# Seven of eight expert quads scattered to rows in memory and gathered back by token, in a GDN + MoE layer on one core

## The chip, the cores and the metric

One core of one Trainium2 chip. The metric is device microseconds for one execution of the whole program, the median of several runs. One execution is taken with the hardware profiler; its time and its span stand beside the runs.

## The reference

One encoder layer over 512 tokens of width 1024, float32: a gated delta mixer, a residual LayerNorm, a hierarchical mixture of experts, a second residual LayerNorm, and a gated projection. The change touches what lies from the first LayerNorm to the second.

```python
x = _layernorm(ALPHA * x + gdn_mixer(x), ln_g[0], ln_b[0])       # ALPHA = 2 ** 0.25
g_onehot = one_hot(argmax(x @ w_group + b_group), 4)             # 1 of 4 groups
e = (x @ w_router + b_router)[chosen group]                      # 8 experts of that group
top_val, top_idx = top_k(e, 2)
top_w = softmax(top_val) * p_group                               # two weights per token
for each chosen expert (w_gate, w_up 1024x256, w_down 256x1024):
    h += top_w * ((silu(x @ w_gate) * (x @ w_up)) @ w_down)
x = _layernorm(ALPHA * x + h, ln_g[1], ln_b[1])
x = x + sigmoid(x @ pe_w_gate) * (p @ pe_w_proj)
```

There are 32 experts and two per token, so 1024 pairs of a token and an expert.

## The kernel before

P is 128 and D 1024; the tokens lie as four chunks `c` of 128 rows in `x1` (also called `z`). The first 700 us or so compute the mixer; there the change only drops four loads and adds a small copy.

**First LayerNorm (`apply`, `store`).** Each chunk is normalised on ACT, given gain and bias by POOL (L859, L860, 128x512 each; one chunk by DVE, L853, L854), stored to the table `x1d` in DRAM (L863), and then scaled by ALPHA on ACT (L865).

**Routing.** A chain of small operations on DVE finds each token's two experts and its slot. The experts form eight quads `q` of four; an expert has 32 slots in each of two tiles `t`, so a quad has 256 slots. `table()` makes the token number of each slot, `gim` (L1083). What doesn't fit its slots goes to an overflow loop over a list (`ntot`, `elist`, `gio`); with these inputs the list is empty. Behind `gim` the same DVE stream computes that list, the two weights `cw` and the weight by quad and token `cq` (L1125 to L1191).

**Experts.** The weights come in 96 tiles of 1 MB, twelve a quad (eight for `up`, four for `down`), through a ring of 16 slots; `load()` (L798, on SP's queue) issues the next tile at each step and waits until its slot is free. `fetch(q)` gathers the 256 rows of a quad from `x1d` with two indirect DMAs on POOL (L952) into a tile `E`, two quads ahead. `flip_x` transposes them, `up` multiplies with gate and up weights, step `kt` of eight (L1223 on PE), while `stage` copies the next tile's four expert blocks into `ws`, three on DVE (L1216) and one on ACT (L1218), with two buffers. `down` multiplies with the down weights, and `split` leaves the result as a high and a low part (L1279, L1280). The result is brought to its tokens by one-hot matrices `oh` (L1268): `combine` makes four matmuls (L1306) for each chunk and half, and `add` accumulates on DVE with the weight `cq` (L1311). These eight pieces of quad q are the list `fill`, one at each step of `up(q + 1)`.

**Order.** From quad 0 on the order on each engine is the order in the code (`in_order`), and so it is in the routing for all but SP. Elsewhere a scheduler sets it.

**Tail.** The gate weights (`w<-in_pe_g`) are split into high and low parts on ACT and POOL (L1405, L1406); then come the second LayerNorm (`norm`, L1412 to L1421) and the gate matmuls L1435. `project_p` (L914, stored as `pjd`) is done early, in pieces around the routing as `NPJ` says.

Of the kernel before, what the change touches and what calls it, by code (L numbers as in the profile page):

```python
# [44 lines left out]
SO = (1, 2, 0, 3)  # L45
TE = 'V'
NPJ = (0, 1, 1)
LNV = (1,)
# [13 lines left out]
TC = 256  # L62


@with_exitstack
def program(ctx: ExitStack, tc: tile.TileContext, a: dict, out: bass.AP):
# [45 lines left out]
    dramp = ctx.enter_context(tc.tile_pool(name="dramp", bufs=1, space=bass.MemoryType.DRAM))  # L112

# [474 lines left out]
    def finish(qt, get):  # L588
# [13 lines left out]
        t = wk.tile([P, 2, NC_, 2], F32, name="rq2")  # L602
# [245 lines left out]
    def apply(c, y, nm, ny):  # L848

        if c in LNV:  # L850
            for n in range(2):
                ns = slice(512 * n, 512 * n + 512)
                V.scalar_tensor_tensor(x1[:, c, ns], x1[:, c, ns], nm, lng[n], op0=OP.add, op1=OP.mult)  # L853
                V.scalar_tensor_tensor(x1[:, c, ns], x1[:, c, ns], y, lng[2 + n], op0=OP.mult, op1=OP.add)  # L854
        else:
            A.activation(x1[:, c], x1[:, c], AF.Identity, bias=ny, scale=y)
            for n in range(2):
                ns = slice(512 * n, 512 * n + 512)
# [28 lines left out]
    for c in SO:  # L887
        store(c)
        if R0 > RA:
            after(stored[-1], early[-1])  # L890
# [57 lines left out]
    def fetch(q):  # L948

        xg = ab_pool.tile([P, 2, D], F32, name="E")  # L950
        for t in range(2):
            i = nc.gpsimd.indirect_dma_start(out=xg[:, t], out_offset=None, in_=x1d[:, :],  # L952
                                         in_offset=bass.IndirectOffsetOnAxis(ap=gim[:, 2 * q + t:2 * q + t + 1], axis=0))
        fetched.append(i)
        return xg
# [107 lines left out]
    def table(slot, col, nm, e):  # L1063
# [19 lines left out]
        V.tensor_copy(gi, gf)  # L1083

        def numbers():
            yf = rtile((16,), "yf")
            V.tensor_scalar(yf, pln[:, 2], 0.0, None, op0=OP.is_equal)
            V.scalar_tensor_tensor(gf, yf, 1.0e5, gf, op0=OP.mult, op1=OP.add)
            if nm == "o":
                V.tensor_scalar(pln[:, 2], pln[:, 2], -1.0, 0.0, op0=OP.add, op1=OP.max)  # L1090
                V.scalar_tensor_tensor(gf, pln[:, 2], 512.0, gf, op0=OP.mult, op1=OP.add)
        return gi, gf, numbers
# [3 lines left out]
    gim, gfm, numbers = table(s128, col, "m", V if TE == "V" else G)  # L1096
# [5 lines left out]
    numbers()  # L1102
# [14 lines left out]
    e2 = rtile((NC_, 1), "e2")  # L1117
    V.tensor_sub(e2, m2, m1)
    A.activation(ge, ge, AF.Exp)
    A.activation(e2, e2, AF.Exp)  # L1120


    NL = 16
    lim = rtile((1, 32), "lim")
    V.tensor_scalar(lim, pre, -32.0, 160.0, op0=OP.mult, op1=OP.add)  # L1125
    V.tensor_scalar(lim, lim, 32.0, None, op0=OP.max)
    nb = rtile((1, 32), "nb")
    V.tensor_sub(nb, prk[:, NC_:], lim)
    nbi = rtile((1, 32), "nbi", I32)
    V.tensor_scalar(nbi, nb, 0.0, 127.0, op0=OP.max, op1=OP.add)  # L1130
    V.tensor_scalar(nbi, nbi, 7, None, op0=OP.arith_shift_right)
    V.tensor_copy(nb, nbi)
    cum = rtile((2, 1, 32), "cum")
    V.tensor_copy(cum[:, 0], nb)
    for j in range(5):
        s_, d_ = cum[:, j % 2], cum[:, 1 - j % 2]
        o = 1 << j
        V.tensor_copy(d_[:, :, :o], s_[:, :, :o])
        V.tensor_add(d_[:, :, o:], s_[:, :, o:], s_[:, :, :32 - o])
    inc = cum[:, 1]  # L1140
    exc = rtile((1, 32), "exc")
    V.tensor_sub(exc, inc, nb)
    ntot = per.tile([P, 1], I32, name="ntot")
    V.tensor_copy(ntot, inc[:, 0, 31:32])
    tlim = rtile((2, NC_), "tlim")
    of_token(tlim, lim.to_broadcast([P, NC_, 32]), t32)
    texc = rtile((2, NC_), "texc")
    of_token(texc, exc.to_broadcast([P, NC_, 32]), t32b)
    V.tensor_sub(tlim, rank, tlim)
    oi = rtile((2, 2, NC_), "bi", I32)  # L1150
    V.tensor_copy(oi[:, 0], tlim)
# [92 lines left out]
    def up(q, xgT, js, ws, fill):  # L1244
# [4 lines left out]
        for kt in range(KT):  # L1249
# [10 lines left out]
            if fill:  # L1260
                fill.pop(0)()
# [9 lines left out]
    def down(q, hT, js, ws, fill, ys):  # L1271
# [11 lines left out]
        for n in range(2):  # L1283
# [14 lines left out]
            if fill and q < 7:  # L1298
                fill.pop(0)()
# [289 lines left out]
```

## Time and profile before

| what | value |
|---|---|
| median of 3 runs | 1116.09 us (1110.93 to 1119.45) |
| the profiled execution | 1118.27 us, its span 1116.5 us |
| busy share of the span | PE 90%, DVE 72%, ACT 49%, POOL 30% |
| mean granted TensorE clock | 0.942 of full |
| from HBM, to HBM | 174.77 MB read, 12.65 MB written |

The stages by the trace: mixer to about 700 us, first LayerNorm to 736, routing to 754, quad 0 from 769, quad 1 from 799, last expert matmul 1038.7, tail to 1116.5. A busy share is a mean over these stages; the sections below read single stages. The granted clock is 1.00 at the 2.4 GHz level and 0.50 at the 1.2 GHz level. A group of "busy, mean ns of one" is followed by the idle time of its engine in front of it and by what ended it.

### The profile page before, as it was taken

How to read it: one execution, taken by the hardware profiler on the slowest of the kernel's cores; microseconds unless marked ns; L12 is line 12 of the kernel's file. 1: busy time of each engine (PE TensorE's matmuls, PEld its weight loads, DVE VectorE, ACT ScalarE, POOL GpSimd, SP SyncE). 2: the span in 40 equal slices, each digit the busy share in tenths (PEclk: the TensorE clock that was granted, in tenths of full speed). 3: DMA queues.
4: the chain of work that ended last, by engine and by line, in shares of the span. 5: the costliest groups of instructions: out<-in, count | busy, mean ns of one | idle time of the engine just before them, and what ended most of it. 6: DMA issues, size and time to landing. Idle time of an engine off the chain costs nothing. (4 is left out here: it accounts for less than half of the span.)

```text
span 1116.5 us, 19701 instructions
## 1 busy us (share of the span) xinstructions
PE 1009.3 (90%) x6954; PEld 703.5 (63%) x6954; DVE 809.4 (72%) x1834; ACT 548.3 (49%) x1406; POOL 334.3 (30%) x273
## 2 busy tenths in 40 slices
PE   9876798977979999989999999958999999999688
PEld 7755677765868887778877888833333333333377
DVE  5889997999894778996556322697666666666784
ACT  3455566655574777556586343224443334432321
POOL 1544534232234344424240274052000000000452
PEclk7988899987999998999999999969999999999789
DMA  4324232121123313223154234878999999970401
GB/s 150 108 66 124 85 98 65 49 57 29 48 90 124 91 58 117 92 77 111 61 161 145 88 123 132 340 274 309 415 420 419 420 406 393 393 319 38 190 28 48
DMA packets 80117, 188.71 MB, mean 169 GB/s; under 512 B 15345, under 2 KB 36849, under 8 KB 67345
## 3 DMA queue, kind: packets, MB, share of 16 engines
q1 hardware_dynamic: 77712, 179.05, 44.1%
q0 software_dynamic: 2304, 8.39, 2.0%
q8 instruction: 55, 0.90, 0.3%
q14 instruction: 46, 0.37, 0.1%
HBM read 174.77 MB, written 12.65 MB: 168 GB/s over the span
## 5 line engine op out<-in xcount | busy, mean ns | idle before, releaser
L240 POOL TENSOR_TENSOR wl<-wr,wh 128x512 fp32r<-128x512 f32 x120 | 160.8, 1343 | 322.8 <-PE pin L243 136.6
L243 PE MATMUL pin<-xh,wh 128*128 128x512 f32 x448 | 137.1, 426 | 36.1 <-DVE cv L257 29.1
L243 PE MATMUL pin<-xl,wh 128*128 128x512 f32 x448 | 135.2, 419 | 0.0
L243 PE MATMUL pin<-xh,wl 128*128 128x512 f32 x448 | 131.2, 412 | 0.3 <-POOL wl L240 0.3
L243 PEld LDWEIGHTS pin<-xh,wh 128*128 128x128 f32 x448 | 86.4, 202 | 57.6 <-DVE cv L257 12.6
L238 ACT ACTIVATE wh<-wr 128x512 fp32r<-128x512 f32 x120 | 75.8, 632 | 92.5 <-PE pin L243 41.2
L1218 ACT ACTIVATE ws<-w 128x512 f32 x96 | 60.5, 630 | 111.8 <-PE ps L1223 57.9
L1216 DVE COPY ws<-w 128x512 f32 x288 | 105.7, 424 | 9.4 <-issue 3.5
L257 DVE SCALAR_TENSOR_TENSOR cv<-pin,cvw,cv 128x510 f32<-128x510 f32 (+1 forms) x128 | 94.4, 741 | 14.8 <-ACT cv L254 14.0
L243 PEld LDWEIGHTS pin<-xl,wh 128*128 128x128 f32 x448 | 89.1, 202 | 19.4 <-DVE xl L642 0.2
L243 PEld LDWEIGHTS pin<-xh,wl 128*128 128x128 f32 x448 | 87.2, 198 | 19.1 <-POOL wl L240 0.7
L952 POOL DMA_INDIRECT E<-x1d,gim x16 | 16.2, 1013 | 170.3 <-PE ps L1206 157.0
L446 POOL TENSOR_TENSOR dc<-dc,negm 128x512 f32<-128x512 f32 x32 | 47.0, 1473 | 44.3 <-DMA dc<-gcd 18.9
L397 DVE TENSOR_TENSOR x<-x,tmp 128x30 f32<-128x30 f32 (+14 forms) x120 | 56.3, 469 | 2.1
L395 DVE TENSOR_TENSOR tmp<-x 128x30 f32<-128x30 f32 (+14 forms) x120 | 53.5, 446 | 2.1
L1311 DVE SCALAR_TENSOR_TENSOR x<-pin,cq,x 128x512 f32<-128x512 f32 x36 | 26.9, 750 | 36.4 <-PE pin L1306 33.0
L448 ACT ACTIVATE dc<-dc,lb 128x128 f32<-128x128 f32 x128 | 41.6, 399 | 15.2 <-POOL dc L446 14.2
L1435 PE MATMUL ps<-w 128*128 128x512 f32 (+1 forms) x192 | 46.4, 405 | 0.0
L542 DVE SCALAR_TENSOR_TENSOR r<-ps,negc,nv 128x128 f32<-128x128 f32 x96 | 29.0, 344 | 23.3 <-PE ps L539 23.1
L1435 PEld LDWEIGHTS ps<-w 128*128 128x128 f32 x192 | 37.5, 206 | 7.6
L1223 PE MATMUL pin<-ws,AT 128*32 128x512 f32 x256 | 39.8, 593 | 0.8 <-DVE ws L1216 0.8
L538 PE MATMUL ps<-st,kcm 128*128 128x256 f32 x96 | 31.7, 413 | 9.6 <-DVE st L570 5.6
(460 smaller groups left out, 2164.7 us busy)
## 6 DMA issues: line engine op xcount, KB each, us to landing
w<-in_w_gu SPq DMA_DIRECT2D x64, 1024.0 KB, 10.0
w<-in_w_dn SPq DMA_DIRECT2D x32, 1024.0 KB, 8.4
wr<-in_w_in SPq DMA_DIRECT2D x96, 256.0 KB, 2.7
dc<-gcd SPq DMA_DIRECT2D x32, 256.0 KB, 3.4
wr<-in_w_out SPq DMA_DIRECT2D x24, 256.0 KB, 3.0
zd<-th SPq DMA_DIRECT2D x16, 256.0 KB, 2.5
zs<-zd SPq DMA_DIRECT2D x16, 256.0 KB, 2.7
w<-in_pe_g SPq DMA_DIRECT2D x6, 512.0 KB, 5.9
```

What stands on the lines that cost most here:

```text
L238: A.activation(wh, wr, AF.Copy)
L240: G.tensor_tensor(wl, wr, wh.bitcast(F32), op=OP.subtract)
L243: T.matmul(ps, w[:, k], parts[k0 + k][n], start=(k0 + k + n == 0 and w is wh), stop=(k0 + k == nk_ - 1 and w is wl))
L257: V.scalar_tensor_tensor(y[:, lo:hi], ps[:, lo + j - 2:hi + j - 2], cvw[:, m, j:j + 1], y[:, lo:hi], op0=OP.mult, op1=OP.add)
L395: V.tensor_tensor(t, X[:, m + 1:, m:m + 1].to_broadcast([P, n, m]), X[:, m:m + 1, :m].to_broadcast([P, n, m]), op=OP.mult)
L397: V.tensor_tensor(X[:, m + 1:, :m], X[:, m + 1:, :m], t, op=OP.add)
L446: G.tensor_tensor(dc, dc, negm[:, d:d + 1].to_broadcast([P, 4, P]), op=OP.add)
L448: A.activation(dc[:, u], dc[:, u], AF.Exp, bias=lb[:, c, u0 + u:u0 + u + 1])
L1216: V.tensor_copy(ws[:, p:p + 1], src)
L1218: A.activation(ws[:, p:p + 1], src, AF.Copy)
L1223: T.matmul(ps[32 * j:32 * j + 32], l[:, 32 * j:32 * j + 32], w[:, j], start=first, stop=last, skip_group_check=True)
L1435: T.matmul(pg[n][:, 0:w], x_[:, kt], w_[kt][:, 512 * n + o:512 * n + o + w], start=(kt == 0 and m == 0), stop=(kt == KT - 1 and m == 2))
```

## The change

Quads 0 to 6 (`MQ` = 7) no longer use the one-hot combine. `down` copies its result on ACT into a tile `yr` (tag `AT`), and two indirect DMAs on POOL scatter the 256 rows to a table `yd` in DRAM, row 256 q + slot. The row numbers `rows_w` of empty slots are out of bounds, and such rows are skipped; the gathers of `fetch` now skip empty slots in the same way. `yd` is filled with zeros by fourteen DMAs of 512 KB on SP's queue; its last row, filled by one more, is what a token reads for a choice that lies in quad 7 or in the overflow list. At quad 7 `collect` gathers for each chunk and each of the two choices the rows of the 128 tokens (eight indirect DMAs), and eight DVE operations add them with the weight `cw`, one at each step of `up(7)`. Quad 7 keeps the combine.

`x1` and `x1d` hold bare normalised rows: gain and bias are applied per feature in `flip_x`, where a feature is a partition (`gbT`), and the residual is put together later by sixteen DVE operations (`residual`), four a quad in quads 3 to 6, from a broadcast of the LayerNorm gain and bias (1 MB, loaded at quad 2).

The list calculations become a generator `later`, of which a piece runs at each step of `up` in quads 0 and 1. `project_p` moves (`NPJ`): two chunks ahead of the rank sums, one ahead of the table, one behind.

```diff
-NPJ = (0, 1, 1)
+NPJ = (2, 3, 3)
+MQ = 7
+    yd = dramp.tile([256 * MQ + 1, D], F32, name="yd")
+    gbT = lgp.tile([P, KT, 2], F32, name="gbT")
+    V.tensor_copy(gbT, wrg[:, :, 36:38])
-    lng = [hd.tile([P, S], F32, name="kkq", bufs=BKK) for _ in range(4)]
-    for i in range(4):
-        nc.sync.dma_start(lng[i], a["ln"][:, i // 2, 512 * (i % 2):512 * (i % 2) + 512].to_broadcast([P, 512]))
     def apply(c, y, nm, ny):
-        if c in LNV:
...
-        else:
-            A.activation(x1[:, c], x1[:, c], AF.Identity, bias=ny, scale=y)
-            for n in range(2):
-                ns = slice(512 * n, 512 * n + 512)
-                G.tensor_tensor(x1[:, c, ns], x1[:, c, ns], lng[n], op=OP.mult)
-                G.tensor_tensor(x1[:, c, ns], x1[:, c, ns], lng[2 + n], op=OP.add)
+        A.activation(x1[:, c], x1[:, c], AF.Identity, bias=ny, scale=y)
     def store(c):
         stored.append(nc.sync.dma_start(x1d[c * P:(c + 1) * P, :], x1[:, c]))
-        A.activation(x1[:, c], x1[:, c], AF.Copy, scale=ALPHA)
...
-                                         in_offset=bass.IndirectOffsetOnAxis(ap=gim[:, 2 * q + t:2 * q + t + 1], axis=0))
+                                         in_offset=bass.IndirectOffsetOnAxis(ap=gim[:, 2 * q + t:2 * q + t + 1], axis=0),
+                                         bounds_check=S - 1, oob_is_err=False)
...
     xg = [fetch(0)]
     for i in range(R1, RA + RB):
         after(load(), fetched[0], True)
+    zer = rt.tile([P, 512], F32, name="zer")
+    G.memset(zer, 0.0)
+    after(nc.sync.dma_start(yd[256 * MQ:, :].rearrange("o (r e) -> o r e", e=512),
+                            zer[0:1, None, :].to_broadcast([1, 2, 512])), fetched[1], True)
+    for i in range(2 * MQ):
+        nc.sync.dma_start(yd[P * i:P * i + P, :].rearrange("p (r e) -> p r e", e=512),
+                          zer[:, None, :].to_broadcast([P, 2, 512]))
...
+    def later():
+        V.scalar_tensor_tensor(yfm, yfm, 1.0e5, VAL[:, 0, 0:1].to_broadcast([P, 16]), op0=OP.mult, op1=OP.add)
+        V.scalar_tensor_tensor(rows_w, IO32[:, 0:16], 128.0, yfm, op0=OP.mult, op1=OP.add)
...
+        V.tensor_scalar(rows_r, no, 256.0 * MQ, None, op0=OP.min)
...
     def flip_x(xg):
...
-            A.activation(xgT[:, 2 * k2:2 * k2 + 2], pt, AF.Copy)
+            for i in range(2):
+                kt = 2 * k2 + i
+                A.activation(xgT[:, kt], pt[:, i], AF.Identity, scale=gbT[:, kt, 0:1], bias=gbT[:, kt, 1:2])
+    def residual(lng):
+        def part(c, n, k):
+            z_ = z[:, c, 512 * n:512 * n + 512]
+            if k:
+                V.scalar_tensor_tensor(z_, lng[:, 2 + n], ALPHA, z_, op0=OP.mult, op1=OP.add)
+            else:
+                V.scalar_tensor_tensor(z_, lng[:, n], ALPHA, z_, op0=OP.mult, op1=OP.mult)
+        return [lambda c=c, n=n, k=k: part(c, n, k) for c in range(NC_) for n in range(2) for k in range(2)]
     def down(q, hT, js, ws, fill, ys):
+        if q < MQ:
+            yr = ab_pool.tile([P, 2, D], F32, name="AT")
         def split(n, py):
+            if q < MQ:
+                for t in range(2):
+                    A.activation(yr[:, t, 512 * n:512 * n + 512], py[t], AF.Copy)
+                return
...
+        for t in range(2 if q < MQ else 0):
+            nc.gpsimd.indirect_dma_start(
+                out=yd[:, :], out_offset=bass.IndirectOffsetOnAxis(ap=rows_w[:, 2 * q + t:2 * q + t + 1], axis=0),
+                in_=yr[:, t], in_offset=None, bounds_check=256 * MQ - 1, oob_is_err=False)
         return ws
+    def collect():
+        gs_ = [ab_pool.tile([P, 2, D], F32, name="E") for _ in range(2)] + [ring([P, 2, D]) for _ in range(2)]
+        for c in range(NC_):
+            for k in range(2):
+                nc.gpsimd.indirect_dma_start(
+                    out=gs_[c][:, k], out_offset=None, in_=yd[:, :],
+                    in_offset=bass.IndirectOffsetOnAxis(ap=rows_r[:, k, c:c + 1], axis=0))
+        def part(c, k):
+            V.scalar_tensor_tensor(z[:, c], gs_[c][:, k], cw[:, k, c:c + 1], z[:, c], op0=OP.mult, op1=OP.add)
+        return [lambda c=c, k=k: part(c, k) for c in range(NC_) for k in range(2)]
...
     for q in range(8):
...
+        fill = []
+        if q < 2:
+            fill = [lambda: next(rest, None) for _ in range(8)]
+        elif q == 2:
+            for _ in rest:
+                pass
...
+            lng = e2.tile([P, 4, 512], F32, name="y")
+            nc.sync.dma_start(lng, a["ln"][:, 0:2].rearrange("o k (n w) -> o (k n) w", n=2).to_broadcast([P, 4, 512]))
+        elif q < 7:
+            fill = res_parts[:4]
+            del res_parts[:4]
+        if q == 2:
+            res_parts = residual(lng)
+        if q == 7:
+            fill = collect()
         h = up(q, xgT, js, ws, fill)
...
-        oh = slots(q)
+        if q >= MQ:
+            oh = slots(q)
...
-        fill = [lambda q=q, c=c, n=n, y=y, oh=oh: add(q, c, n, combine(oh, y, c, "ps1" if q % 2 else "pin"))
-                for n, y in enumerate(ys) for c in range(NC_)]
```

On DVE, between the routing and the first staging copies of quad 0, the end of the list calculations (`hot` and `ef` to `elist`, `gp`, `den`) stands ahead of the copies before:

```order
L1167 TENSOR_REDUCE ef<-hot 128x16
L1169 CAST ei<-ef 128x16
L1171 TENSOR_SCALAR elist<-ei 128x16
L1172 TENSOR_SCALAR elist<-ei 128x16
L1175 TENSOR_REDUCE gp<-ge 128x4
L1177 SCALAR_TENSOR_TENSOR den<-e_7768,gp 128x4
L1216 ISA
L1216 COPY ws<-w 128x512
```

In the changed kernel the copies on DVE come at once behind `gim` and the choice of the quads' experts, `jsel`:

```order
L1082 CAST gim<-gfm 128x16
L1104 TENSOR_TENSOR t_7660<-ROW,pre 128x32x3
L1108 TENSOR_REDUCE jr<-t_7660 128x32
L1110 CAST jsel<-jr 128x32
L1114 TENSOR_TENSOR ge<-lg,mxg 128x16
L1116 TENSOR_TENSOR e_7765<-mx_7601,mx_7589 128x4
L1263 TENSOR_LOAD jsel
L1263 ISA x6
L1242 ISA
L1242 COPY ws<-w 128x512
```

Some fifty operations moved behind these copies, into the steps of quads 0 and 1.

On POOL, from the first LayerNorm to the end of the overflow list's load, the program before has gain and bias (`kkq`), the gathers, and the split of a gate weight tile (`w<-E,w`):

```order
L859 TENSOR_TENSOR x_66<-x_66,kkq 128x512 x2
L860 TENSOR_TENSOR x_66<-x_66,kkq 128x512 x3
L952 DMA E<-x1d,gim 128x1024 x2
L1070 TENSOR_TENSOR B_7814<-cols,VAL 128x384
L952 DMA E<-x1d,gim 128x1024 x14
L1406 TENSOR_TENSOR w<-E,w 128x1024 x2
L1315 TENSOR_LOAD ntot
```

In the changed kernel POOL has, from the scatters of quad 5 on, with the semaphores that each waits for (DMASW are those of POOL's own DMAs):

```order
L1343 DMA yd<-AT,rows_w 1793x1024 [waits DMASW7_49,Activation_49]
L1343 DMA yd<-AT,rows_w 1793x1024 [waits DMASW2_49,Activation_49]
L1343 DMA yd<-AT,rows_w 1793x1024 [waits DMASW4_49,DMASW3_49,Activation_49]
L1343 DMA yd<-AT,rows_w 1793x1024 [waits DMASW5_49,DMASW4_49,Activation_49]
L1353 DMA E<-yd,rows_r 128x1024 [waits DMASW5_49,PE_49]
L1353 DMA E<-yd,rows_r 128x1024
L1353 DMA E<-yd,rows_r 128x1024 [waits DMASW1_49,DMASW0_49,PE_49]
```

Scatters and collecting gathers took the place of the splits, which now follow behind the overflow loop.

On DVE in `up(7)` of the changed kernel an addition of collected rows, which waits for its gather, stands between the staging copies of two steps:

```order
L1242 ISA
L1242 COPY ws<-w 128x512
L1358 SCALAR_TENSOR_TENSOR x_66<-E,cw,x_66 128x1024 [waits DMASW6_49]
L1242 ISA
L1242 COPY ws<-w 128x512 [waits DMAHW5_49,DVE_49,PE_49]
```

Before, an addition of combined results, 128x512 and fed by PE, stood at that place (`x_66<-pin,cq,x_66`).

## Rows read from the trace of the kernel before

**Rows 1.** Windows: length, busy of PE, PEld, DVE, ACT, POOL, granted clock, DMA share, GB/s.

```profile
730.00:740.00 10.00, 2.68 (x16) 2.65 (x17) 9.48 (x33) 3.45 (x4) 6.60 (x7) 0.69 0.52 169
740.00:750.00 10.00, 4.35 (x10) 2.22 (x10) 9.24 (x39) 0.16 (x1) 3.47 (x3) 0.50 1.00 382
750.00:760.00 10.00, 9.27 (x29) 3.90 (x28) 6.97 (x38) 4.72 (x7) 2.13 (x2) 0.96 0.67 237
760.00:770.00 10.00, 6.92 (x37) 3.34 (x35) 8.27 (x28) 6.60 (x12) 3.60 (x3) 0.89 0.81 304
780.00:990.00 210.00, 208.25 (x1511) 77.25 (x1503) 139.59 (x322) 82.04 (x149) 10.10 (x10) 1.00 1.01 410
1001.00:1020.00 19.00, 19.00 (x140) 6.82 (x140) 12.14 (x29) 6.43 (x11) 0.00 (x0) 1.00 0.14 57
730.00:1001.00 271.00, 251.45 (x1733) 96.70 (x1733) 187.72 (x499) 105.17 (x188) 27.97 (x26) 0.96 0.96 384
```

**Rows 2.** Groups by line within quad 1, 798.7 to 832.99 us.

```profile
L1216 DVE COPY ws<-w 128x512 f32 x36 | 13.3, 426 | 0.6 <-issue 0.4 <-PE ps L1223 0.2
...
L1311 DVE SCALAR_TENSOR_TENSOR x<-pin,cq,x 128x512 f32<-128x512 f32 x8 | 6.0, 751 | 8.4 <-PE pin L1306 7.5 <-issue 0.9
...
L1306 PE MATMUL pin<-y,oh 128*128 128x512 f32 x16 | 4.8, 420 | 0.0
...
L1279 ACT ACTIVATE y<-ps 128x512 fp32r<-128x512 f32 x2 | 1.2, 597 | 0.5 <-PE ps L1223 0.5
```

**Rows 3.** Timeline of quad 1, one contraction step to the next.

```profile
801.68 1.06 PE L1223 MATMUL ps<-w,AT 128*32 128x512 f32 x8
...
803.54 1.19 PE L1306 MATMUL pin<-y,oh 128*128 128x512 f32 x4
...
804.66 0.64 PE L1223 MATMUL ps<-w,AT 128*32 128x512 f32 x4
```

**Rows 4.** DMA issues, 690 to 1010 us: KB each, median us to landing.

```profile
w<-in_w_gu SPq DMA_DIRECT2D x64, 1024.0 KB, 10.0
w<-in_w_dn SPq DMA_DIRECT2D x32, 1024.0 KB, 8.4
...
E<-x1d,gim POOLq DMA_INDIRECT x16, 9.5
```

**Rows 5.** The gather line L952 alone, all sixteen.

```profile
DMA to landing us min/median/max: 5.2/9.5/12.4
```

**Rows 6.** Waits of SP's queue, 690 to 1010 us.

```profile
SPq L798 <- PE ps L1223: 82.9, 48, 2.2
```

**Rows 7.** Timeline, end of the first LayerNorm to the first staging copies.

```profile
737.28 2.48 POOL L859 TENSOR_TENSOR x<-x,kkq 128x512 f32<-128x512 f32 x2 [1.37 <-ACT x L856]
...
737.42 1.15 DVE L973 TENSOR_TENSOR ohg<-ohg,kmg 128x16 f32<-128x16 f32 x1
...
744.75 0.19 DVE L973 TENSOR_TENSOR oh<-oh,km 128x32 f32<-128x32 f32 x1
...
746.04 6.03 PE L914 MATMUL pin<-E,AT 128*128 128x512 f32 x8
...
753.66 0.17 DVE L1083 CAST gim<-gfm 128x16 int32<-128x16 f32 x1
...
754.13 1.19 POOL L952 DMA_INDIRECT E<-x1d,gim  x1 [10.66 <-DVE yf L1087]
...
770.97 0.76 DVE L1216 COPY ws<-w 128x512 f32 x2 [0.17 <-issue]
```

**Rows 8.** Timeline, last expert matmuls to the first norm behind the loop.

```profile
1037.66 1.04 PE L1223 MATMUL ps<-ws,hT 128*32 128x512 f32 x8
...
1045.08 2.30 SPq L1392 DMA_DIRECT2D w<-in_pe_g  x5
...
1050.08 5.10 POOL L1406 TENSOR_TENSOR w<-w 128x1024 fp32r<-128x1024 f32 x2 [9.86 <-ACT w L1405]
...
1050.13 2.84 DVE L1421 SCALAR_TENSOR_TENSOR x<-x,ly,E 128x512 f32<-128x512 f32 x1
```

More of the change, by code (lines that the diff above doesn't have):

```diff
@@ L601, in finish @@
         f = wk.tile([P, 2, NC_, 2], F32, name="ff")
-        t = wk.tile([P, 2, NC_, 2], F32, name="rq2")
+        t = wk.tile([P, 2, NC_, 2], F32, name="rq2", bufs=1)
         rsqrt(f, ms, t)
@@ L1082, in table @@
         gi = per.tile([P, 16], I32, name="gi" + nm)
[L1083 to L1092, printed above, removed]
+        if nm == "o":
+            V.tensor_copy(gi, gf)
+        yf = rtile((16,), "yf")
+        V.tensor_scalar(yf, pln[:, 2], 0.0, None, op0=OP.is_equal)
+        V.scalar_tensor_tensor(gf, yf, 1.0e5, gf, op0=OP.mult, op1=OP.add)
+        if nm == "o":
+            V.tensor_scalar(pln[:, 2], pln[:, 2], -1.0, 0.0, op0=OP.add, op1=OP.max)
+            V.scalar_tensor_tensor(gf, pln[:, 2], 512.0, gf, op0=OP.mult, op1=OP.add)
+        else:
+            V.tensor_copy(gi, gf)
+        return gi, gf, yf
     for c in range(NPJ[1], NPJ[2]):
         project_p(c)
-    gim, gfm, numbers = table(s128, col, "m", V if TE == "V" else G)
+    gim, gfm, yfm = table(s128, col, "m", V if TE == "V" else G)
     xg = [fetch(0)]
@@ L1116, in program @@
     V.tensor_tensor(ge, gl, gm.to_broadcast([P, NC_, 4]), op=OP.subtract)
-    e2 = rtile((NC_, 1), "e2")
-    V.tensor_sub(e2, m2, m1)
+    e2x = rtile((NC_, 1), "e2")
+    V.tensor_sub(e2x, m2, m1)
     A.activation(ge, ge, AF.Exp)
-    A.activation(e2, e2, AF.Exp)
+    A.activation(e2x, e2x, AF.Exp)
     NL = 16
[L1124 to L1139, printed above, removed]
@@ L1259, in up @@
                 jss.append(quad_js(q + 1))
-            if fill:
+            for _ in range(-(-len(fill) // (KT - kt))):
                 fill.pop(0)()
@@ L1320, in overflow @@
             ii = per.tile([P, 1], I32, name="ii")
-            V.tensor_copy(ii, gio[:, bass.ds(i, 1)])
+            V.tensor_copy(ii, lists[0][:, bass.ds(i, 1)])
             ff = per.tile([P, 2], F32, name="ff")
-            V.tensor_copy(ff[:, 0:1], gfo[:, bass.ds(i, 1)])
+            V.tensor_copy(ff[:, 0:1], lists[1][:, bass.ds(i, 1)])
             V.tensor_scalar(ff[:, 1:2], ff[:, 0:1], -512.0, None, op0=OP.add)
@@ L1331, in overflow @@
                     T.transpose(pt[:, k], xg[:, (4 * n + k) * P:(4 * n + k + 1) * P], ident)
-                A.activation(xt[:, n].rearrange("p (k t) -> p k t", k=4), pt, AF.Copy)
+                    kt = 4 * n + k
+                    A.activation(xt[:, n, k * P:(k + 1) * P], pt[:, k], AF.Identity, scale=gbT[:, kt, 0:1],
+                                 bias=gbT[:, kt, 1:2])
             pg = PT([P, 512], "ps2")
@@ L1360, in overflow @@
                                                op1=OP.add)
-    e2 = t2.enter_context(tc.tile_pool(name="e2", bufs=1, side="right", reuse_waits="tile"))
     pcs = {}
@@ L1458, in program @@
     jss = [quad_js(0)]
-    fill = []
+    rest = later()
+    lng = None
     for q in range(8):
@@ L1465, in program @@
             ws = stage(ready[0], js)
+        fill = []
[4 more added lines that the diff above has]
+                pass
+            rts.close()
+            e2 = t2.enter_context(tc.tile_pool(name="e2", bufs=1, side="right", reuse_waits="tile"))
+            lng = e2.tile([P, 4, 512], F32, name="y")
[7 more added lines that the diff above has]
+            fill = collect()
         h = up(q, xgT, js, ws, fill)
```

147 lines of the change are left out of this document (87 added, 60 removed).

## The prediction

> **What bounds the kernel now.** I read the windows first [rows 1]. From 780 to 990 us, six quads of experts, PE is busy 208.25 of 210.00 us at a granted clock of 1.00, and the DMA engines are full too (1.01, 410 GB/s). Two busy resources do not both pace, so I went to the queue that issues the weight loads: its longest sum of waits is 82.9 us in 48 waits on PE's expert matmuls L1223, each for a ring slot that PE has not yet freed [rows 6]. So PE paces and the DMA only just keeps up. The end agrees: in 1001 to 1020 us the DMA share is 0.14 and PE is busy all 19.00 us [rows 1], and the last expert matmul starts at 1037.66 [rows 8]. PE is some 37 us behind its last weights.
>
> Where PE's time goes: within quad 1 one contraction step lasts 804.66 − 801.68 = 2.98 us, of which the combine L1306 of the quad before (four matmuls) takes 1.19 [rows 3]. The other place is the routing, 730 to 770 us: PE is busy 2.68 and 4.35 us of the first two tens, the DMA share is 0.52, 1.00, 0.67, 0.81 [rows 1], and DVE's small operations make the chain. The list calculations stand in front of the staging copies, which only start at 770.97, though the gather was issued at 754.13 [rows 7].
>
> **The change part by part.** *Combines.* Eight a quad go for quads 0 to 6: 8 × 1.19 = 9.5 us of PE a quad, with DVE's eight additions of 0.751 [rows 2, 3]. A quad of 34.29 us (quad 1's window in [rows 2]) falls to about 24.8 on PE. The weights do not arrive faster, so this is a gain only until the DMA paces: twelve tiles of 1.049 MB are 12.58 MB, at 410 GB/s [rows 1] 30.7 us a quad, with one MB of gather and scatter 32 to 33. So PE catches up, uses up its lead of 16 tiles by about quad 5, and then waits. What goes is PE's lag behind the DMA, 37 us, not 7 × 9.5 = 67.
>
> *When the last tile before quad 7 lands.* Before, 271 us at 384 GB/s from 730 to 1001 [rows 1] are 104.1 MB. To that the zero fill adds 7.34 MB, the LayerNorm gain and bias 1.05, the scatters of quads 0 to 5 (781 occupied rows of 4 KB, counted from the routing of the reference's inputs) 3.20; the gathers lose 1024 of 2048 rows, 4.19. Sum 111.5 MB; less quad 7's 12.58, 98.9. At 410 to 423 GB/s (the 1.01 windows read 410; I allow 3% more for fewer gather packets) that is 234 to 241 us. The idle of the DMA in 730 to 770 (0.48 + 0 + 0.33 + 0.19 of ten us, 10 us) shrinks to perhaps 4, since the loads behind the gather start earlier and the zeros fill the rest. So the last tile of quad 6 lands at 968 to 975; I take 971. Costed as hidden, the zero fill alone would be nothing: it would be so if PE still paced. Here it is paid in full, 7.34/0.410 = 18 us.
>
> *Routing.* The removed gain and bias operations of POOL (L859, L860, about 1.24 each) run beside DVE's chain, and a DVE operation that takes 0.19 us alone took 1.15 there [rows 7]. Without them some 8 us of routing go (an estimate: five or six operations so stretched by 1 us each, and a few in the LayerNorm ahead): gather index at about 746 instead of 753.66, quad 0 from 760 instead of 769, and the copies no longer behind the lists. That lets PE start its catching up; the DMA decides later, so I put nothing more into the sum than the earlier loads. What DVE takes up instead, the lists in quads 0 and 1 and sixteen additions of 0.75 in quads 3 to 6, lies beside PE: a step has three copies of 0.426 on DVE [rows 2] against 2.7 us of arrival. If that cover went, 16 × 0.75 = 12 us would show.
>
> *The collection in quad 7, the added wait.* On POOL the two scatters of quad 6 stand one behind the other's completion, and the first gather behind the last scatter's; the gather's reader is an addition on DVE, in order, with the staging copies of step 1 of quad 7 onward behind it. PE waits for those. So from 971: copy, matmuls and evictions of the last tile 0.76 + 2 × 1.06 + 2 × 0.6, so 975 [rows 2, 3, 7]; then three indirect transfers. The gathers of before land in 5.2 to 12.4 us, median 9.5 [rows 5], about as long as the loads of 1 MB beside them, 8.4 to 10.0 [rows 4]. I take 7.5 for 82 rows, 6 for 11 rows, 9.5 for the full one, 23 together (bounds 3 × 5.2 = 16 and 3 × 12.4 = 37): the first addition at 998. A sentence by itself: the Trainium skill, "DMA: Bandwidth & Descriptors", section on the anatomy of one DMA (SWDGE), fits 2.0 us plus bytes at 436 GB/s, an estimate of 3.2 us for 128 rows of 4 KB, which would make the three under 10 us and the end some 13 us earlier, 1091, beside rival A. With that fit the trace of before disagrees: no gather here landed under 5.2.
>
> From there DVE paces quad 7's up part: eight additions of 128x1024 (an estimate of 1.3, bounded by 2 × 0.75) and six groups of three copies of 0.43, 8 × 1.3 + 6 × 1.1 = 17; the first copies come early, so 16 to PE's end of up. Down is the rest of a quad: 34.29 − 8 × 2.98 = 10.4. End of the expert matmuls: 998 + 16 + 10.5 = 1024.5, against 1038.7 (1037.66 + 1.04) [rows 8]: −14.
>
> *Tail.* The splits of the gate weights on POOL (5.10 us for two) ran partly before the loop's end, and one behind it stretched an addition of 0.75 to 2.84 [rows 8]; now all come behind the loop. I take +2.5 (0 to +6).
>
> **Sum.** −14 + 2.5 = −11.7 on the profiled 1118.27, which stands 2.2 above the median of 1116.09; so 1106.5 against the profile and **1104** against the median.
>
> **Rivals.** *A: the chain is light.* The three transfers land at 5.2, 5.2 and 7.5 (18 us, not 23) because most slots are skipped, and the engines stay at 423 GB/s (−4 us), and the tail loses nothing (−2.5): 1104 − 11.5 = 1092. For it: the smallest landing of [rows 5], and quad 6 scatters 93 rows of 256. Against it: the engines are full when these are issued.
>
> *B, slower: the chain of three.* Each of scatter, scatter and gather takes the longest landing or more. At 12.4 each they make 37 us, +14: 1118; with the last tile at 975 too, 1122. From about 14 us each with that late tile (1122 + 3 × 1.7 = 1127) the kernel is slower by over 1%. For it: a scatter is a write that no row of the trace shows, behind eight loads in flight, and three must follow one another; against it: 82 and 11 rows are less than 128.
>
> *C: the clock falls while PE waits for weights.* In 740 to 750 us PE was busy 4.35 of ten and the granted clock read 0.50, the 1.2 GHz level; there eight matmuls L914 took 6.03 us, 0.75 each against 0.42 for the same width at full clock [rows 1, 2, 7]. A step of 2.98 − 1.19 = 1.79 us would become 1.79 × 0.75/0.42 = 3.2, longer than the arrival of 2.7: +0.5 for the 16 or so tiles that are left when PE has caught up, +8: 1112. The Trainium skill, "TensorE: Matmul & The Clock Gate", section on HAM oscillation, describes this: where the compute on a tile is shorter than the wait for the next one, each tile starts at the lower clock. Against it in this trace: 0.89 in 760 to 770 with PE busy 6.92 of ten [rows 1], and here PE would be busy about 1.8 to 2.1 of 2.7.
>
> *D: the skipped slots are not cheaper.* If transfers of out-of-range rows still cost their time, 1024 gathered and 918 scattered rows, 8.0 MB at 410 GB/s or 19 us, come back, nearly all of it ahead of the last tile of quad 6: +18: 1122. It is the case in which the change does not do what it says. Against: a row that isn't moved has no bytes.
>
> **How the numbers follow.** One per cent, about what a measurement of this kernel can tell from no change, is 11 us: 1105 and 1127. The forecast (1099 to 1110) has 0.45, A 0.18, C 0.15, B 0.15, D 0.07. Faster by over 1%: half of the forecast and a little more (0.25), A all of it, and the lighter ends of B and C (0.05): 0.48. Slower: 0.05 of B and 0.05 of D, and 0.02 for two of them together: 0.12. The rest, 0.40, is within 1%. The range is 1088 to 1121: it takes in A and C and B up to 12.4 us each, and leaves the worst of B and D out.
>
> **What would show it.** In the profile of the changed kernel: no combine in quads 0 to 6 and a step of quad 1 at about 1.8 to 2.1 us; gather index at 744 to 748; from quad 5 on PE idle until loads land, at a DMA share of 1.00; the last tile of quad 6 at 968 to 975; then a gap on PE of some 25 us at the start of quad 7, with DVE waiting for a gather into E; the last expert matmul at 1020 to 1029. I am wrong if the DMA share falls under 0.95 in quads 1 to 5, if the scatters land in under 4 or over 13 us, or if the clock reads 0.50 in quads 5 and 6.

## The result, and the profile after

The changed kernel takes 1121.88 us (median of 20 runs), the kernel before 1116.1 (20 runs): ratio 1.0052, 95% interval 1.0032 to 1.0071. It is half a per cent slower, where 1104 was forecast and the range ended at 1121. The span of its profiled execution is 1125.2 us.

Windows of the changed kernel, columns as in [rows 1]: two tens of the routing, the stretch from inside quad 3 to inside quad 6, the end of quad 6, and the start of quad 7.

```profile
740.00:750.00 10.00, 6.26 (x19) 2.49 (x17) 9.04 (x49) 2.39 (x4) 0.00 (x0) 1.00 0.97 364
750.00:760.00 10.00, 5.40 (x16) 2.30 (x16) 3.01 (x13) 2.02 (x5) 4.72 (x5) 0.83 1.02 402
864.50:968.90 104.40, 87.68 (x664) 26.62 (x656) 50.70 (x129) 43.91 (x85) 13.47 (x13) 0.97 1.02 418
975.00:1000.00 25.00, 18.90 (x152) 6.06 (x147) 8.98 (x25) 12.45 (x25) 0.98 (x1) 1.00 1.01 413
1000.00:1010.00 10.00, 0.00 (x0) 0.00 (x0) 0.00 (x0) 0.00 (x0) 0.97 (x1) 0.50 0.63 261
1010.00:1020.00 10.00, 0.00 (x0) 0.00 (x0) 1.44 (x2) 0.00 (x0) 7.68 (x8) 0.50 0.80 274
```

The DMA engines are full from 740 us on, and in the long stretch too (1.02, 418 GB/s), as forecast. PE now has idle time there (busy 87.68 of 104.40 us), at a clock of 0.97. From 1000 to 1020 us PE does nothing at all.

The timeline of ACT, the first activation of each quad's gate half, which marks the end of `up` in quads 1 to 7:

```profile
822.64 0.39 ACT L1268 ACTIVATE h<-ps 128x256 f32<-128x256 f32 x1 [2.27 <-PE ps L1259]
...
848.13 0.38 ACT L1268 ACTIVATE h<-pin 128x256 f32<-128x256 f32 x1 [1.87 <-PE pin L1259]
...
874.09 0.39 ACT L1268 ACTIVATE h<-ps 128x256 f32<-128x256 f32 x1 [0.44 <-PE ps L1259]
...
909.38 0.39 ACT L1268 ACTIVATE h<-pin 128x256 f32<-128x256 f32 x1 [0.44 <-PE pin L1259]
...
944.46 0.38 ACT L1268 ACTIVATE h<-ps 128x256 f32<-128x256 f32 x1 [0.44 <-PE ps L1259]
...
978.68 0.39 ACT L1268 ACTIVATE h<-pin 128x256 f32<-128x256 f32 x1 [0.44 <-PE pin L1259]
...
1032.69 0.38 ACT L1268 ACTIVATE h<-ps 128x256 f32<-128x256 f32 x1 [2.40 <-PE ps L1259]
```

Quad 2 takes 848.13 − 822.64 = 25.5 us: that is a quad without combines while PE still has a stock of tiles. Then the stock is used up, and quads 4, 5 and 6 take 35.3, 35.1 and 34.2 us. Before, a quad took 34.3 [rows 2]. PE no longer has the 9.5 us of combines to do in each of them, and yet the quads are no shorter.

The timeline around the end of quad 6, then the end of the experts:

```profile
987.59 1.10 DVE L1242 COPY ws<-w 128x512 f32 x3 [1.33 <-DMA w<-in_w_dn]
...
991.88 0.98 POOL L1343 DMA_INDIRECT yd<-AT,rows_w  x1 [22.28 <-ACT AT L1317]
...
1001.54 0.97 POOL L1343 DMA_INDIRECT yd<-AT,rows_w  x1 [8.69 <-issue]
1010.18 0.98 POOL L1353 DMA_INDIRECT E<-yd,rows_r  x1 [7.67 <-DMA yd<-AT,rows_w]
...
1018.56 1.28 DVE L1358 SCALAR_TENSOR_TENSOR x<-E,cw,x 128x1024 f32<-128x1024 f32 x1 [24.79 <-DMA E<-yd,rows_r]
...
1019.77 1.14 DVE L1242 COPY ws<-w 128x512 f32 x3
...
1020.24 2.65 PE L1259 MATMUL ps<-ws,AT 128*32 128x512 f32 x8 [24.27 <-DVE ws L1242]
```

```profile
1044.48 1.04 PE L1259 MATMUL ps<-ws,hT 128*32 128x512 f32 x8
...
1052.37 3.90 SPq L1452 DMA_DIRECT2D w<-in_pe_g  x6
```

The weight tiles are numbered from 0, twelve a quad; the first row is the staging copy of tile 83, the last of quad 6. Scatter, scatter and gather follow one behind the other, 991.88 to 1018.56; DVE waits 24.79 us for the gather, and PE 24.27 us for DVE's copies behind it. The last expert matmul ends at 1045.5; before it was 1038.7 [rows 8].

The DMA issues from 690 to 1060 us (columns as in [rows 4]), and the landings of the scatters alone:

```profile
w<-in_w_gu SPq DMA_DIRECT2D x64, 1024.0 KB, 21.7
w<-in_w_dn SPq DMA_DIRECT2D x32, 1024.0 KB, 22.2
yd<-zer SPq DMA_DIRECT2D x14, 512.0 KB, 8.7
...
yd<-AT,rows_w POOLq DMA_INDIRECT x14, 8.3
```

```profile
DMA to landing us min/median/max: 7.7/8.3/9.7
```

### The profile page after: what moved, and what is told of

It reads as the page before. It is cut to its first block, busy times and chain, and to the rows that moved or that the text cites. A ratio compares the mean times of both kernels' runs of the same rounds, so it can differ in the third digit from the quotient of the medians.

```text
span 1125.2 us, 19316 instructions
## 1 busy us (share of the span) xinstructions
PE 963.7 (86%) x6730; PEld 676.9 (60%) x6730; DVE 759.3 (67%) x1762; ACT 557.5 (50%) x1435; POOL 340.5 (30%) x284
## 5 line engine op out<-in xcount | busy, mean ns | idle before, releaser
L1343 POOL DMA_INDIRECT yd<-AT,rows_w x14 | 14.3, 1023 | 199.0 <-ACT AT L1317 112.6
L1259 PE MATMUL ps<-ws,AT 128*32 128x512 f32 x256 | 43.2, 619 | 24.3 <-DVE ws L1242 24.3
L449 ACT ACTIVATE dc<-dc,lb 128x128 f32<-128x128 f32 x128 | 41.5, 397 | 16.8 <-POOL dc L447 15.8
L1259 PE MATMUL pin<-ws,AT 128*32 128x512 f32 x256 | 43.4, 627 | 3.7 <-DVE ws L1242 3.7
L1495 PE MATMUL ps<-w 128*128 128x512 f32 (+1 forms) x192 | 44.1, 390 | 0.0
L1259 PE MATMUL pin<-w,AT 128*32 128x512 f32 x256 | 37.5, 620 | 6.6 <-DMA w<-in_w_gu 6.5
L1259 PE MATMUL ps<-w,AT 128*32 128x512 f32 x256 | 38.8, 623 | 3.9 <-DMA w<-in_w_gu 3.9
```

Of the source, the lines that this page charges most:

```text
L449: A.activation(dc[:, u], dc[:, u], AF.Exp, bias=lb[:, c, u0 + u:u0 + u + 1])
L1259: T.matmul(ps[32 * j:32 * j + 32], l[:, 32 * j:32 * j + 32], w[:, j], start=first, stop=last, skip_group_check=True)
L1495: T.matmul(pg[n][:, 0:w], x_[:, kt], w_[kt][:, 512 * n + o:512 * n + o + w], start=(kt == 0 and m == 0), stop=(kt == KT - 1 and m == 2))
```

## The experiments

Twelve kernels ran, all timed beside the kernel before. Times are medians; where a staging time is given "behind the index", it is counted from the gather index `gim` of the same profile, since that came anywhere from 742.4 to 755.2 us in them; a difference of two such times is free of where the routing ended. In the changed kernel it came at 752.20, so tile 83 was staged 235.4 us behind it.

**The zero fill moved into the mixer.** Zeros go to the first chunk at the start, and thirteen copies in memory follow the stores of the mixer's gate input; the fill behind the routing is gone.

```diff
+    nc.sync.dma_start(yd[0:P, :]..., zf[:, None, :].to_broadcast([P, 4, 256]))
...
         st_ = nc.sync.dma_start(z_dram[h], th)
+        if 0 < h < 2 * MQ:
+            after(nc.sync.dma_start(yd[P * h:P * h + P, :], yd[0:P, :]), st_)
```

> The changed kernel, but the table yd is filled with zeros during the mixer (first chunk from a zero tile at the start, thirteen more copied in memory, one behind each of thirteen stores of the gate input), where the DMA engines are mostly idle; nothing is filled behind the routing. Theory A (from quad 1 on the DMA engines pace, so each MB that lands in quads 0 to 6 is paid in full): 7.34 MB at 417 GB/s are 17.6 us; the last tile of quad 6 is staged at about 970 instead of 987.6 us, the time is 1104 (1100 to 1109). Rival B (the fill fills engine time that would have been idle, and only the chain of scatters and gather at quad 7 costs): 1119 to 1124.

1106.44 us, ratio to before 0.9921 (0.9889 to 0.9953). DVE's timeline, tile 83's copy and the first addition:

```profile
962.07 1.10 DVE L1240 COPY ws<-w 128x512 f32 x3 [1.03 <-DMA w<-in_w_dn]
...
993.26 1.28 DVE L1356 SCALAR_TENSOR_TENSOR x<-E,cw,x 128x1024 f32<-128x1024 f32 x1 [24.93 <-DMA E<-yd,rows_r]
```

With the index at 746.63, tile 83 is staged 215.4 us behind it, 20 us earlier. Theory A holds: the fill was paid nearly in full, 15.4 us of time for 17.6. The gap in front of the first addition stays (24.93 us), so the two costs are separate. Leaving the fill out altogether was not tried, since the gathers would then read a table of which part is unwritten.

**The additions behind the expert matmuls.**

```diff
-            fill = collect()
+            coll = collect()
...
+    for f in coll:
+        f()
     between()
```

> The changed kernel, but the eight additions of collected rows stand on DVE behind the expert matmuls of quad 7, not between the staging copies of up(7); gathers and scatters are issued as before. Theory A (loads are late, and the in-order wait of DVE for the first gather stops PE for 24 us): PE's gap at the start of quad 7 goes, the last expert matmul is set by the last loads and comes at about 1020 instead of 1044.5; the eight additions of 1.28 us then come behind it: 1107 (1101 to 1113). Rival B (quad 7 waits for its weights anyway, since its loads land behind the gathers): within 4 us of 1122.

1111.75 us, 0.9962 (0.9936 to 0.9989): inside theory A's range, near its slow end. The timeline:

```profile
1017.18 1.04 PE L1259 MATMUL ps<-ws,hT 128*32 128x512 f32 x8
...
1019.61 5.11 DVE L1358 SCALAR_TENSOR_TENSOR x<-E,cw,x 128x1024 f32<-128x1024 f32 x4
...
1024.64 5.12 DVE L1358 SCALAR_TENSOR_TENSOR x<-w,cw,x 128x1024 f32<-128x1024 f32 x4
```

With the index at 746.35, PE ends its experts at 1018.2, 271.9 us behind it instead of 293.3: the gap is worth 21.4 us, as theory A has it. But the additions, 10.2 us, then stand ahead of everything in the tail, and the time falls by 10 only.

**Four loads in flight for eight.**

```diff
...
+            if len(issued) >= 20:
+                after(ld, issued[-4], True)
...
```

> The changed kernel, but from the twentieth weight tile on each load waits until the load four before has landed, so that four and not eight are in flight. Theory A (loads in flight share the engines, so when the last tile of quad 6 lands some four of the next tiles have been moved too): a load lands in about 11 us instead of 21.7, the last tile of quad 6 is staged some 5 us earlier at the same GB/s, time 1117 (1113 to 1120). Rival B (loads are served in the order of issue): landing times halve, but the tile is staged when it was, time 1120 to 1124. Rival C (four in flight don't keep the engines full): DMA share under 0.97 in quads 1 to 6, slower than 1126.

1121.74 us, 1.005 (1.0023 to 1.0077). A window over quads 1 to 6, and the landing of a load:

```profile
780.00:975.00 195.00, 165.90 (x1293) 52.35 (x1291) 103.94 (x277) 90.18 (x175) 24.00 (x23) 0.96 1.00 399
```

```profile
w<-in_w_gu SPq DMA_DIRECT2D x64, 1024.0 KB, 11.3
```

A load lands in 11.3 us, the engines move 399 GB/s for 417 in the same window of the changed kernel, and tile 83 is staged 236.7 us behind the index, 1.3 later than there. Theory A said earlier, C a share under 0.97 and slower than 1126: neither. Rival B said all three numbers: landing times halved, the tile staged when it was, 1120 to 1124. The mean rate fell by 4% and the tiles came hardly later, so the mean rate is not what lands tiles.

**Empty slots gathered too.** The index is taken before the empty slots are put out of bounds.

> The changed kernel, but the gathers of a quad's rows fetch the empty slots as well (as row 0), as before the change; the scatters still skip them. Theory A (a skipped row costs nothing, and a moved one 4 KB of a full engine): 1024 rows or 4.19 MB more, nearly all ahead of the last tile of quad 6, are 9 to 10 us: 1131 (1128 to 1134). Rival D (a skipped row costs as much as a moved one): 1120 to 1124.

1123.96 us, 1.0078 (1.0049 to 1.0107). POOL's queue in 690 to 1060 us, packets, MB and share, in the changed kernel and here:

```profile
q0 software_dynamic: 5472, 11.98, 8.7%
```

```profile
q0 software_dynamic: 5472, 16.17, 11.3%
```

A skipped row moves next to no bytes (4.19 MB between the two, at the same number of packets). But those 4.19 MB cost 5 us of arrival (tile 83 at 240.4), not the 10 of theory A, and the time lies in rival D's range: 2 us above the changed kernel, with overlapping intervals. By arrival, half of theory A is there; by time, that skipping saves anything is not shown.

**Plain stores of whole quads, no zero fill.** Each quad stores its 256 rows, empty slots too, with two plain DMAs on POOL's queue.

> The changed kernel, but without the zero fill (only the one last row is filled), and each quad stores all its 256 rows, empty slots too, with two plain DMAs on POOL's queue in place of the scatters; no store waits for the one before. Theory A: ahead of the last tile of quad 6 7.34 MB go and about 3.1 MB come, 4.2 MB or 10 us; and the chain at quad 7 has one transfer less, another 9 to 10 us: 1102 (1097 to 1108), the first addition at about 998 instead of 1018.6. Rival B (only the chain costs, the fill is hidden): 1112 (1109 to 1115).

1105.73 us, 0.9894 (0.9833 to 0.9955): inside theory A's range, and below rival B's. Tile 83 is staged 220.1 us behind the index, and the first addition 27.0 us behind that (31.0 in the changed kernel): one wait less in the chain saves 4 us, since the plain stores, 512 KB each, land in 10.2.

**Both mended.** Early fill, and the additions behind the matmuls (those of chunks 2 and 3 behind the first norm).

> Both mended: yd is filled with zeros during the mixer, and the additions of collected rows stand behind the expert matmuls of quad 7 (those of chunks 0 and 1 at once, those of 2 and 3 behind the first norm). Theory A: PE ends its experts some 3 us behind the last loads, at about 995 us in a profile whose gather index comes at 746, and the tail is longer by the additions: 1106.4 less 20 us of the gap and of DVE's pacing, plus 6: 1092 (1088 to 1097). Rival B (the gathers end last anyway, and the additions only move): 1102 to 1107.

1102.82 us, 0.9861 (0.9811 to 0.9911): at the lower end of rival B's range, and not in theory A's. Against the profile of the early fill alone the last expert matmul comes 14.6 us earlier behind the index (258.7 for 273.3), but the tail is 10.7 us longer (90.3 for 79.6), so the additions in the tail give back most of the gap, and the time is only 3.6 us lower.

**Quad 7's loads, from its second on, held back until tile 83 has landed.**

```diff
...
+            if len(issued) == 85:
+                after(ld, issued[83], True)
...
```

> The changed kernel, but the load of tile 85 (the second of quad 7) is issued only when tile 83, the last of quad 6, has landed; tiles 85 to 95 stand behind it in the queue. Theory A (loads in flight share the engines, so that 4.7 MB of quad 7 are moved before tile 83 is complete): tile 83 is staged 8 to 10 us earlier, at about 226 us behind the gather index instead of 235; the scatters and the gather meet emptier engines and land in 5 to 7 us; time 1108 (1103 to 1113). Rival B (loads are served in the order of issue, and only the chain gets lighter): staged at 235 still, time 1115 to 1119. Rival C (what is held back is missing later): 1122 or more.

1122.53 us, 1.0062 (1.0038 to 1.0086). Three views: the issue of tile 83, the issue of tile 85 (which is tile 83's landing), and the windows between.

```profile
L799 SPq DMA_DIRECT2D w<-in_w_dn x1: 328/328/328, 963.1 to 963.1; - x1
```

```profile
984.57 4.04 SPq L799 DMA_DIRECT2D w<-in_w_gu  x7
```

```profile
965.00:970.00 5.00, 4.19 (x32) 1.23 (x32) 2.83 (x7) 1.26 (x2) 1.00 (x1) 1.00 1.01 420
970.00:975.00 5.00, 3.48 (x27) 0.71 (x24) 1.44 (x4) 0.99 (x2) 0.00 (x0) 1.00 0.65 268
975.00:980.00 5.00, 4.02 (x32) 1.81 (x28) 3.02 (x10) 3.25 (x9) 0.00 (x0) 1.00 0.26 107
980.00:985.00 5.00, 5.00 (x48) 1.62 (x44) 2.22 (x8) 3.98 (x9) 0.00 (x0) 1.00 0.14 59
985.00:990.00 5.00, 5.00 (x48) 1.51 (x44) 1.93 (x6) 3.18 (x7) 0.98 (x1) 1.00 0.93 315
```

This is the row that I lacked. From 975 to 985 us the engines move (107 + 59) × 5 us = 0.83 MB, and in 980 to 985 their share is 0.14, about two of sixteen; yet tile 83, issued at 963.1, lands only at 984.57, 235.3 us behind the index, the same as ever. Theory A (sharing) falls; the staging time is rival B's, the total is rival C's. The windows suggest that a tile has landed when its last part has, and that a few engines are far behind the rest.

The traces hold sixteen completions of every load, which I read as one for each engine's part; the last is the landing. They bear it out (us; tile 36 is the first of quad 3):

| load | first | eighth | twelfth | last | apart |
|---|---|---|---|---|---|
| changed kernel, tile 36 | 842.1 | 845.5 | 846.2 | 848.9 | 6.8 |
| changed kernel, tile 83 | 970.8 | 974.4 | 977.3 | 987.5 | 16.7 |
| held back, tile 83 | 968.7 | 970.6 | 974.3 | 984.4 | 15.8 |
| four in flight, tile 83 | 975.6 | 976.1 | 977.0 | 980.1 | 4.5 |
| early fill, tile 83 | 945.2 | 950.8 | 952.4 | 962.0 | 16.7 |
| plain stores, tile 83 | 956.6 | 960.0 | 962.1 | 966.5 | 9.9 |

Twelve of tile 83's sixteen parts were there 10 us before the last. The engines that are ahead run on into the next tiles, which is why the mean share and GB/s look full. With four loads in flight they can't run far ahead (4.5 us apart), so the mean rate falls, and the last part comes when it did.

**Six quads scattered.** Quad 6 is combined in `up(7)`; no scatter stands ahead of the gathers.

> The changed kernel with six quads scattered and not seven: quad 6 too is combined by one-hot matmuls, in up(7) between the additions of collected rows, so that the last scatter is that of quad 5 and no scatter stands between the last tile of quad 6 and the gathers. Theory A (the gap of 24 us at the start of quad 7 comes from the chain of two scatters and a gather): the gap falls to under 4 us, up(7) takes 3.1 us a step for 2.35 (DVE: 1.09 of copies, 1.28 and 0.75 of additions), and the zero fill is 1 MB smaller: 1122 less 22, 3 and plus 7: 1104 (1099 to 1110). Rival B (the first gather waits for something else): 1120 or more.

1107.07 us, 0.9907 (0.9875 to 0.9939). DVE's timeline at the start of quad 7:

```profile
989.04 1.29 DVE L1242 COPY ws<-w 128x512 f32 x3
...
991.03 1.33 DVE L1358 SCALAR_TENSOR_TENSOR x<-E,cw,x 128x1024 f32<-128x1024 f32 x1
...
996.48 1.27 DVE L1358 SCALAR_TENSOR_TENSOR x<-E,cw,x 128x1024 f32<-128x1024 f32 x1
```

The first addition comes 2 us behind a staging copy, without waiting for its gather. Theory A holds.

**No indirect transfers in the later quads.** Scatters of quads 1 to 6 are left out, and plain loads of x rows replace the gathers of quads 2 to 7, so that the output is not the layer's.

> A measurement of the pace of the weight loads: the changed kernel without the indirect transfers of quads 2 to 6. The scatters of quads 1 to 6 are left out, and the rows of quads 2 to 7 are read from the table x1d with plain DMAs on SP's queue, always the first 256 rows. Theory S (the loads themselves land at 2.87 us a tile, since a tile has landed only when the slowest of the sixteen engines has its part): a quad stays at 34 to 35 us in quads 3 to 6, and the last tile of quad 6 is staged within 3 us of 235 behind the gather index. Theory I (the indirect transfers slow some engines): a quad takes 32.5 us or less, the tile is staged at 228 or earlier. The time falls in both, since no scatter of quad 6 stands ahead of the gathers: 1104 to 1110 by S, under 1100 by I.

1111.87 us, 0.9974 (0.9955 to 0.9994). The same marks as above, quads 4 to 6:

```profile
903.08 0.39 ACT L1271 ACTIVATE h<-pin 128x256 f32<-128x256 f32 x1 [1.86 <-PE pin L1262]
...
936.82 0.39 ACT L1271 ACTIVATE h<-ps 128x256 f32<-128x256 f32 x1 [1.86 <-PE ps L1262]
...
970.55 0.39 ACT L1271 ACTIVATE h<-pin 128x256 f32<-128x256 f32 x1 [1.86 <-PE pin L1262]
```

Quads 5 and 6 take 33.7 us each, quad 4 903.08 − 865.46 = 37.6, and tile 83 is staged 242.1 us behind the index, later than either theory allows. But here the quads don't measure the loads. PE's first transposes of x rows for quads 4 and 7, ahead of matmuls of `down`:

```profile
875.65 0.45 PE L1233 MATMUL ps<-cst,E 128*128 128x128 f32 x1 [8.67 <-DMA E<-x1d]
...
978.21 0.45 PE L1233 MATMUL ps<-cst,E 128*128 128x128 f32 x1 [6.33 <-DMA E<-x1d]
```

The landing of tile 83's load, issued at 953.5, and its staging copy:

```profile
DMA to landing us min/median/max: 22.4/22.4/22.4
```

```profile
987.90 1.10 DVE L1245 COPY ws<-w 128x512 f32 x3 [0.64 <-PE ps L1262]
```

PE waits for the plain loads of x rows, which stand in SP's queue behind weights (30.7 us in all), and tile 83 lies landed for 12 us before it is staged. It landed at 975.8, 230.0 us behind the index, between the two theories: 5.4 us earlier than in the changed kernel, of which some 1.4 (an estimate: 0.6 MB less ahead of it, at 418 GB/s) are bytes. From tile 48 to tile 83 twelve tiles landed in 33.1 us on average, for 33.9 in the changed kernel, and tile 83's parts were 8.0 us apart, for 16.7. So the indirect transfers have a part in the lag, and the loads alone have one. The time lies above both theories' ranges, since neither had the wait for x rows in it.

**Four quads scattered, and combines from quad 4 on.**

> Four quads scattered; quads 4 to 7 are combined by one-hot matmuls as before the change, and all sixteen residual additions stand in quad 3. The fill behind the routing is 4.2 MB for 7.34. Theory S (from quad 3 on a quad takes 34.5 us because the loads land at that pace, so that the 9.5 us of combine that the change took from PE are worth nothing there): quads 4 to 6 take 34 to 35 us with the combine too, quad 7 as with six quads, and the smaller fill gives back 2.1 MB at 2.6 us: 1107 less 5: 1102 (1097 to 1107). Rival P (PE's time counts there): quads 5 and 6 take over 38 us, 1115 or more.

1099.15 us, 0.9846 (0.9802 to 0.9889). The marks of quads 4 to 7:

```profile
896.93 0.38 ACT L1268 ACTIVATE h<-pin 128x256 f32<-128x256 f32 x1 [0.44 <-PE pin L1259]
...
933.87 0.38 ACT L1268 ACTIVATE h<-ps 128x256 f32<-128x256 f32 x1 [2.52 <-PE ps L1259]
...
968.56 0.38 ACT L1268 ACTIVATE h<-pin 128x256 f32<-128x256 f32 x1 [4.38 <-PE pin L1259]
...
1003.92 0.38 ACT L1268 ACTIVATE h<-ps 128x256 f32<-128x256 f32 x1 [4.84 <-PE ps L1259]
```

Quads 5 to 7, each with eight combines, take 36.9, 34.7 and 35.4 us, against 35.1 and 34.2 without (quads 5 and 6 of the changed kernel). Taking the combine out of those quads bought 2.3 us in quads 5 and 6 together, for the 19 of PE that it freed. Putting it back, with a fill of 4.2 MB for 7.3 and no scatter ahead of the gathers, makes the kernel 23 us faster than the changed one. Theory S holds; rival P (over 38 us a quad) falls.

**Early fill with six and with four quads.**

> Six quads scattered and the zero fill during the mixer (the two edits that gained most, together). If the gains add, the fill's share now 6/7 of 15.5: 1107 less 14: 1093 (1088 to 1098). If both took away the same wait: 1104 or more.

1089.85 us, 0.978 (0.9732 to 0.9827).

> Four quads scattered, combined from quad 4 on, and the fill (4.2 MB) during the mixer. By theory S the same as with six quads and the early fill, within 5 us: 1093 (1088 to 1098), for the early quads run ahead of the loads and the late ones wait for them either way. By rival P: 1105 or more.

1090.62 us, 0.9782 (0.9739 to 0.9824). The gains add (1122 less 15.4 and 14.8 is 1092), and six or four quads make no difference. Both beat the kernel before by 2.2% (intervals from 1.7 to 2.7%).

## Why the prediction was wrong

- **The step that failed** is the landing of tile 83: 98.9 MB at 410 to 423 GB/s make 234 to 241 us, and with it 12.58 MB and one more at that rate make 32 to 33 us a quad. It takes a tile as landed when the mean engine has moved its bytes. I had put the index at 746 and tile 83 at 971, 225 us behind it. It came at 235.4, and at 234.9 to 236.7 in the second, third and hold-back experiments: 10.4 us of the miss. The mean rate was as I read it (418 GB/s in the long window). What it does not tell is when a tile is complete. At 403 GB/s from 730 to 987.5 us 103.8 MB were moved, 4.9 more than the 98.9: parts of quad 7's tiles that came ahead of tile 83's last. From tile 36 to tile 83 the first parts advanced by 128.7 us, 32.9 for twelve tiles, the pace that I forecast; the last parts took 138.6 us, 35.4 for twelve.
- It had a consequence that I did not see. At 34 to 35 us, arrival is no faster than the PE pace of before, 34.3. The combines cost PE 9.5 us a quad, and behind them the loads of the changed kernel came no faster.
- **The zero fill** was forecast at 18 us and cost 15.4 us of time and 20 of arrival (first experiment): right in size.
- **The chain in quad 7** was the right mechanism: scatters, gather, DVE in order, PE waiting 24.27 us (forecast 25). Its size was 991.88 to 1018.56, 26.7 us for 23, and 4.3 us stand between tile 83's staging and the first scatter, for 4. I had made the scatters cheaper for their few rows (7.5 and 6 us); those of a quad's first 128 slots (82 to 106 rows) landed in 8.3 to 9.7 us, those of the second (7 to 66 rows) in 7.7 to 8.4, so rows hardly mattered. The part of rival B that says three transfers must follow one another was right; its 12.4 us each were not.
- **Behind the gather** I forecast 26.5 us to the end of the experts; it was 1045.5 − 1018.56 = 27.0. The tail was 79.7 us behind that against 77.8 before: +1.9 for +2.5.
- **Rival C** did not come: the granted clock was 0.97 in the long window, with PE waiting for tiles; it read 0.83 in 910 to 920 and in 945 to 955 us, and 0.50, the 1.2 GHz level, in the gap of 1000 to 1020. The Trainium skill, "TensorE: Matmul & The Clock Gate", section on HAM oscillation, speaks of tiles whose compute is shorter than the wait for the next one. This case doesn't test it, since PE was busy 87.68 of 104.40 us, far more than it waited.
- **Rival D** is half answered by the fourth experiment: the skipped rows move no bytes to speak of, but gathering all 1024 of them cost 5 us of arrival and 2 of time, not the 10 that the prediction's price per MB gives. The skipped rows of the scatters were not moved in any run.
- **The routing** came out as forecast, as far as it can be told: the index came at 742.4 to 749.2 in the eight other profiles with the same mixer, around the 746 forecast, and at 752.20 in the changed kernel's own. The reason given for it stands open: the two rows compared, 1.15 and 0.19 us, are of one line but of different tiles, and no run put the operations on POOL back.

In sum, 1104 + 10.4 (arrival) + 4.0 (to the first addition: 3.7 of chain, 0.3 ahead of it) + 0.5 (behind the gather) − 0.6 (tail) = 1118; the other 4 us of the median are not accounted for. In the profiled execution, which lies 5 us above the median, the index was 6.2 us late, and with it the sum closes: from the 1106.5 that was forecast against a profile, 1106.5 + 6.2 + 10.4 + 4.0 + 0.5 − 0.6 = 1127.0, and 1126.95 was measured.

Which engines are late, and why, stays open: the completions don't name their engines. The Trainium skill, "DMA: Bandwidth & Descriptors", section "Latency and other measured facts", says that two of the sixteen, 7 and 15, are usually slower, with a guess at POOL's descriptor rings as the cause. The share of 0.14 in 980 to 985 us, while two of tile 83's sixteen parts were still out, agrees with two of sixteen. What feeds the lag is in part the transfers that this change brought: without a fill behind the routing, tile 83's parts were 16.7 us apart with scatters and 9.9 with plain stores; with the fill they were 16.7 apart in the changed kernel and 8.0 without indirect transfers in the later quads. Why a scatter does that, no run shows.

## What to carry to other kernels

When an edit takes work from the engine that paces, price what paces next from its own completions, not from bytes over mean GB/s: a full mean rate can hide a few late engines, and a tile is there only when its last part is. If PE and the loads both read as full, assume that they pace alike until a quad without the one has been seen.

A write and a read through memory form a chain of landings, and an in-order engine that waits for its end stops all that stands behind it; leave at least one stage of other work between the last write and the first read. And fill or clear tables where the DMA engines are idle, not in the stage that they pace.

## What the runs showed that I had not expected

- With eight loads in flight the parts of one tile landed up to 19 us apart (tile 72 of the changed kernel, 938.8 to 957.8), with four 4.5 (tile 83). When later loads were held back, the share fell from 1.01 to 0.65, 0.26 and 0.14 in steps of 5 us, and the tile still took until the end of them.
- The landing of a scatter beside full load queues hardly depends on its rows: 8.3 to 9.7 us for 82 to 106, 7.7 to 8.4 for 7 to 66.
- 4.19 MB more of gathered rows cost 5 us of arrival, 7.34 MB of plain fill 20: a megabyte did not have one price. The parts of tile 83 were 12.9 us apart with the rows gathered and 16.7 without, so part of those bytes may have gone to engines that were ahead; that is a reading, not a test.
